# Another written order for the steps of the four mixers in a two-block transformer kernel

## The chip, the cores and the metric

The kernel runs on one core of a Trainium2 chip. The metric is the device time of one execution in microseconds (us); lower is better.

## What is computed

Two blocks act on 512 tokens of 1024 features, in float32. The first block has two layers. Each is a half-weighted SwiGLU network, a mixer, and a second half-weighted SwiGLU network (width 2816):

```python
x = x + 0.5 * swiglu(rmsnorm(x), gate, up, down)
x = x + mixer(rmsnorm(x) @ w_in) @ w_out
x = x + 0.5 * swiglu(rmsnorm(x), gate, up, down)
```

The mixer of layer 0 ("ab") puts a differential attention of 4 heads beside an RWKV-7 recurrence of 8 heads. The mixer of layer 1 ("cd") puts a sparse attention of 8 heads beside an mLSTM of 4 heads. The second block has two layers, each a mixer ("z0", "z1") and a gated network with a causal convolution. Its mixer joins four parts: HGRN2 (4 heads), gated linear attention (4 heads), latent attention (4 heads) and a gated delta rule (4 heads). Every recurrence is computed in chunks of 128 tokens. The delta rules need the inverse of a triangular 128x128 matrix for each head and chunk.

## The kernel before

Everything lives in the core's own memory; only weights, constants and tables are read while it runs. Each weight arrives as a "unit" of 128 x 1024 float32 (512 KB). `wload` issues its transfer on the queue of SyncE (SP) into one of three buffers named `raw`, used in turn. ScalarE (ACT) then rounds it into `whi` (L440) and VectorE (DVE) puts the rest into `wlo` (L442); these are three buffers each, also used in turn. Where a unit is to be kept, the parts are `khi` and `klo` instead. The activations are split the same way into `hi` and `lo`. A product takes three matmuls for each 128 features: hi*whi, lo*whi and hi*wlo. A unit of a wide projection (`fm`, L383, 8 steps over the features) is thus 24 matmuls of 128 x 512; a token-major one (`tm`) has two units and 96 matmuls of 128 x 256.

The networks are long runs of such units. The mixers are chains of small operations that wait for each other, among which wide projections are placed. A chain is a Python generator that puts down some instructions and yields; a step is what lies between two yields. The string of a mixer in `ORDER` names the chain whose next step is put down:

```python
def run(order, make):
    live = {}
    for n in order.split() + list(make):
        if n not in live:
            live[n] = make[n]()
        next(live[n], None)
```

A chain that has ended ignores further steps. The names of "ab" are:

- `p0` to `p3`: `rwkv_prep`, for each pair of heads three wide projections and the preparation of the recurrence (tiles `xm`, `zw`, `pb`).
- `c0` to `c3`: `rwkv_core`, 20 steps for each pair of heads. Steps 2 to 12 hold the triangular inverse (`tri_inv`: `py`, `pz` on PE; `X` on DVE), and steps 15 to 18 the scan over chunks (`pu`, `pS` on PE; `u`, `S` on DVE and ACT).
- `d`: `diff_proj`, eight wide projections with their rotation (`rot`) and then two token-major ones.
- `a`: `diff_attn`, 19 steps: scores (`sc`), transposes (`pT`), values (`po`), then `on` and `oT`. After steps 9 and 18 one half of the tokens is ready for the output projection.
- `o` and `L`: the output projection. `o` takes the part of the features that comes from the recurrence, in 8 steps of 12 matmuls. `L` (`out_last`) takes the other part: step 1 for tokens 0 to 255 and step 2 for tokens 256 to 511, 48 matmuls each, followed for every 128 tokens by the normalisation for the next network (`xn` on DVE, `xT` on PE).

In "cd", `m` and `y` are the mLSTM, `n` the sparse attention, `v`, `g`, `c`, `z` projections. In "z0" and "z1", `g0`, `g1` are the delta rule (22 steps, tiles `dec`, `py`, `pz`, `pu`, `pS`), `h0`, `h1` HGRN2 and `l` the gated linear attention (12 steps, tiles `gw`, `gpa`, `gpo`), `m` the latent attention (24 steps: `mq`, `sc`, `pT` of `mee`, `mpo`). Wide projections are `a0`, `a1` (two units each), `mp` (three), `lp` (two), `dz0`, `dz1`, `ag0`, `ag1`, `bg0`, `bg1` (one) and the token-major `ai` and `bv`.

The written order is not the order on the engines. The program is built with

```python
with tile.TileContext(nc, schedule_with_timeline_sim=True, auto_bufs=True) as tc:
```

so a planner takes it. It runs the instructions against its own durations and picks, for each engine, among those whose inputs it holds to be ready. Its trial runs, which also settle the buffers, pick the one written first; its last run picks the one that is due first by the times of the trial. The written order also sets which of the three `raw` buffers a unit gets, so units keep their written order among themselves. SP's constants and tables are pinned in written order. On the chip each engine then runs its own list in order.

Of the kernel before, what the change touches and what calls it, by code (L numbers as in the profile page):

```python
# [39 lines left out]
class Layout:  # L40
# [134 lines left out]
    def weights(self):  # L175
# [104 lines left out]

ORDER = {
# [18 lines left out]
}  # L300


# [1747 lines left out]
```

## Time and profile before

| quantity | value |
|---|---|
| median of 3 runs | 3824.14 us (3816.77 to 3828.89) |
| the profiled execution, its own time | 3819.23 us |
| its span, first to last instruction | 3817.4 us |
| TensorE (PE) busy with matmuls | 3700.3 us, 97% |
| TensorE's mean granted clock | 0.963 of full speed |
| VectorE, ScalarE, GpSimd busy | 48%, 37%, 7% |

Outside its span the profiled execution has 3819.23 - 3817.4 = 1.8 us. A granted clock of 1.00 is 2.4 GHz and one of 0.50 is 1.2 GHz; a value between is a stretch that has both. In time, "ab" lies at about 424 to 850 us, "cd" at 1640 to 1930, "z0" at 2310 to 2690 and "z1" at 3085 to 3455.

### The profile page before, as it was taken

The numbers are of one execution on the slowest core, as the hardware profiler recorded it, in microseconds if no ns is written. First come the engines' busy times: TensorE is split into PE (matmuls) and PEld (weight loads), VectorE is DVE, ScalarE is ACT, GpSimd is POOL, SyncE is SP. The second block draws the span as 40 slices with busy tenths as digits, with TensorE's granted clock in tenths as the row PEclk, the third lists the DMA queues.
The fourth block names the chain that finished last, engine by engine and source line by source line (L and its number), as shares of the span: only waits on it lengthen the run. The fifth ranks groups of instructions, "written<-read, shape, count | busy, mean of one in ns | idle before, by whom it ended". The sixth has DMA issues, their size and how long they took to land.

```text
span 3817.4 us, 62093 instructions
## 1 busy us (share of the span) xinstructions
PE 3700.3 (97%) x26572; PEld 3023.7 (79%) x26572; DVE 1824.0 (48%) x3017; ACT 1420.5 (37%) x2557; POOL 277.6 (7%) x314
## 2 busy tenths in 40 slices
PE   8999999999999999999999999999999999999999
PEld 7888877778888888877688887767888887678887
DVE  4334645453334333646533357465534664665345
ACT  3223423342223222535432246345332464453323
POOL 0000211100000000010000003121000021210000
PEclk9999999889999999999999999879999999799999
DMA  3223201202222222411022231201222312012222
GB/s 134 100 95 110 74 29 37 67 29 92 96 96 98 100 94 100 137 67 67 1 97 97 99 111 56 65 18 51 83 100 94 127 51 69 20 51 83 94 100 88
DMA packets 88403, 302.97 MB, mean 79 GB/s; under 512 B 9920, under 2 KB 11840, under 8 KB 88128
## 3 DMA queue, kind: packets, MB, share of 16 engines
q1 hardware_dynamic: 88128, 299.01, 22.8%
q8 instruction: 208, 3.41, 0.4%
q14 instruction: 67, 0.55, 0.0%
HBM read 296.87 MB, written 2.10 MB: 78 GB/s over the span
## 4 chain that ended last, share of the span: by engine, by line
PE 88%; DVE 5%; issue 3%; ACT 2%; DMA 1%; POOL 0%; SPq 0%; DVEq 0%; POOLq 0%; ACTq 0%
PE fm L383 54%; PE dn L383 17%; PE tm L383 3%; PE sc L383 2%; PE pu L383 2%; PE ocat L383 1%; PE pT L387 1%; DMA raw<-in_wts_dram 1%; PE gpa L383 1%; PE xT L387 1%; PE py L383 1%; PE pz L383 1%; PE gpo L383 1%; DVE xn L587 0%; DVE klo L442 0%
## 5 line engine op out<-in xcount | busy, mean ns | idle before, releaser
L442 DVE TENSOR_TENSOR wlo<-raw,whi 128x1024 fp32r<-128x1024 f32 x437 | 539.4, 1234 | 981.3 <-ACT whi L440 979.6
L383 PE MATMUL fm<-hi,whi 128*128 128x512 f32 x2456 | 976.2, 398 | 2.8 <-DVE dec L1772 2.8
L383 PE MATMUL fm<-lo,whi 128*128 128x512 f32 x2456 | 970.5, 395 | 0.0
L383 PE MATMUL fm<-hi,wlo 128*128 128x512 f32 x2456 | 968.8, 394 | 0.0
L440 ACT ACTIVATE whi<-raw 128x1024 fp32r<-128x1024 f32 x437 | 463.1, 1060 | 1354.8 <-PE fm L383 596.7
L383 PEld LDWEIGHTS fm<-hi,whi 128*128 128x128 f32 x2456 | 468.9, 191 | 103.6 <-DVE dec L1772 3.0
L383 PEld LDWEIGHTS fm<-hi,wlo 128*128 128x128 f32 x2456 | 468.3, 191 | 97.4
L383 PEld LDWEIGHTS fm<-lo,whi 128*128 128x128 f32 x2456 | 468.3, 191 | 96.9 <-issue 1.0
L383 PE MATMUL dn<-wlo,hi 128*128 128x512 f32 x768 | 299.0, 389 | 0.0
L383 PE MATMUL dn<-whi,lo 128*128 128x512 f32 x768 | 299.0, 389 | 0.0
L383 PE MATMUL dn<-whi,hi 128*128 128x512 f32 x768 | 299.0, 389 | 0.0
L563 POOL TENSOR_TENSOR smalls<-smalls,mhalf 128x1 f32<-128x1 f32 x60 | 42.5, 709 | 2478.0 <-DVE smalls L562 2471.9
L607 DVE TENSOR_TENSOR silu<-silu,fm 128x512 f32<-128x512 f32 x88 | 60.5, 687 | 312.3 <-PE fm L383 312.3
L383 PE MATMUL fm<-lo,khi 128*128 128x256 f32 x640 | 181.5, 287 | 2.2 <-DVE lo L593 2.2
L383 PE MATMUL fm<-hi,khi 128*128 128x256 f32 x640 | 180.5, 288 | 1.0 <-ACT hi L390 0.7
L383 PE MATMUL fm<-hi,klo 128*128 128x256 f32 x640 | 180.5, 285 | 0.0
L383 PEld LDWEIGHTS dn<-whi,lo 128*128 128x128 f32 x768 | 144.2, 188 | 29.9
L383 PEld LDWEIGHTS dn<-whi,hi 128*128 128x128 f32 x768 | 144.2, 188 | 29.8
L383 PEld LDWEIGHTS dn<-wlo,hi 128*128 128x128 f32 x768 | 144.2, 188 | 29.8
L442 DVE TENSOR_TENSOR klo<-raw,khi 128x512 fp32r<-128x512 f32 x184 | 117.4, 684 | 32.5 <-ACT khi L440 32.4
L383 PEld LDWEIGHTS fm<-lo,khi 128*128 128x128 f32 x640 | 123.8, 194 | 4.1 <-DVE lo L593 3.6
L440 ACT ACTIVATE khi<-raw 128x512 fp32r<-128x512 f32 x184 | 103.8, 622 | 59.6 <-DMA raw<-in_wts_dram 56.1
(544 smaller groups left out, 5428.8 us busy)
## 6 DMA issues: line engine op xcount, KB each, us to landing
raw<-in_wts_dram SPq DMA_DIRECT2D x529, 512.0 KB, 3.3
w<-in_small_dram SPq DMA_DIRECT2D x16, 256.0 KB, 5.4
x<-in_x_dram SPq DMA_DIRECT2D x4, 512.0 KB, 6.5
out_dram<-x SPq DMA_DIRECT2D x4, 512.0 KB, 2.6
ffa_norm<-in_small_dram SPq DMA_DIRECT2D x4, 256.0 KB, 6.7
mix_norm<-in_small_dram SPq DMA_DIRECT2D x4, 256.0 KB, 4.1
ropetab<-in_rope_dram SPq DMA_DIRECT2D x4, 256.0 KB, 4.2
ffb_norm<-in_small_dram SPq DMA_DIRECT2D x4, 256.0 KB, 5.6
```

What stands on the lines that cost most here:

```text
L383: self.nc.tensor.matmul(out, lhsT=lhsT, rhs=rhs, start=start, stop=stop, skip_group_check=True)
L387: self.nc.tensor.transpose(out, in_, self.ident[:p, :p])
L440: nc.scalar.activation(t, raw[:, b:e], AF.Copy)
L442: nc.vector.tensor_sub(lo, raw[:, b:e], hi.bitcast(F))
L563: self.nc.gpsimd.tensor_tensor(r, v, self.mhalf, op=OP.pow)
L607: nc.vector.tensor_mul(s, s, pu)
```

## The change

The four strings of `ORDER` are replaced; each has the same names, each as often as before (123, 91, 127 and 127 of them). No other line differs.

- "ab": `c0` is written up to four steps ahead of `c1` instead of in turn with it, and `c2` and `c3` in runs of two or three steps. `p2` comes one step of `c1` earlier. The first three `d` come 3 to 6 steps of `c0` earlier, the sixth to eighth 2 to 4 steps of `c2` later. The tenth `d` comes after step 18 of `c3` instead of step 16. The last three steps of `o` come after step 11 of `a` instead of step 9. Step 1 of `L` comes after step 18 of `a`, straight before step 2, instead of before step 10.
- "cd": three of the `m` steps and one `n` change places by one or two.
- "z0": `a1` moves from before step 3 of `g1` to before its step 10. The first two steps of `o` come after steps 2 and 3 of `m` instead of step 1, the next four one to three steps of `m` later; some `h` and `g` steps change places by one or two.
- "z1": `a1` moves behind step 4 of `g0`. The first six steps of `o` move later in the same way, the last two come one step of `m` earlier, and step 1 of `L` comes after step 16 of `m` instead of 15.

```diff
     "ab":
-        "p1 p0 c0 c1 c0 c1 c0 c1 c0 c1 c0 c1 p2 c0 c1 c0 c1 c0 c1 c0 c1 d c0 c1 c0 c1 c0 c1 c0 c1 d c0 c1 c0 "
-        "c1 c0 c1 c0 c1 d c0 c1 c0 c1 p3 c0 c1 c2 c3 c2 c3 d c2 c3 c2 c3 c2 c3 d c2 c3 c2 c3 d c2 c3 c2 c3 "
-        "c2 c3 d c2 c3 c2 c3 d c2 c3 c2 c3 d c2 c3 c2 c3 d c2 c3 c2 c3 a c2 c3 a c2 c3 a a o a o a o a o a o "
-        "a o o o L a a a a a a a a a a L",
+        "p1 p0 c0 c1 c0 c1 c0 c1 c0 c0 c1 p2 c0 c1 d c0 c1 c0 c1 c1 c0 c0 d c0 c1 d c0 c1 c0 c1 c0 c0 c1 c1 c0 c1 c0 "
+        "c1 p3 c0 c1 c2 c3 c2 c3 c1 c0 c1 c0 c1 c1 d c2 c2 c2 c3 c3 c3 d c2 c2 c3 c3 c2 c2 c3 c2 c2 d c2 c3 c2 c3 c3 "
+        "c3 c2 d d c3 c3 d c2 c3 c2 c3 c2 c3 c2 c2 c3 d a c3 a c2 c3 a a o o a o a a a a o o a a o o o a a a a a a a "
+        "L L a",
     "cd":
-        "m v m m m v m z m z m m z c m c z m c z m c z c z c n m m n m c m m m n n c m m n m g n m n g g n n "
-        "g n n n n y n n o n o n o n o n o n o o o L n n n n n n n n n n n n n n n n n n L",
+        "m v m m m v m z m z m m z c m c m z m c z m c z c z c n n m m m c m m n n c m m n m g n m n g g n n g n n n "
+        "n y n n o n o n o n o n o n o o o L n n n n n n n n n n n n n n n n n n L",
     "z0":
-        "g0 ai g1 a0 g0 g1 g0 a1 g1 g0 g1 g1 g0 g1 mp g0 g1 g0 lp g0 g1 g1 g1 g0 bv g1 g0 dz0 g1 g0 h1 h1 g0 "
-        "h0 g0 g1 dz1 g0 g1 h0 ag1 g1 h1 h0 g0 h0 h1 g1 g0 h0 g1 h1 g0 g1 h0 h0 h0 h1 g0 g1 ag0 bg0 g0 h1 g0 "
-        "h0 g1 bg1 g1 h1 h1 h1 g0 h1 h0 g0 h0 g1 h0 l h1 m o o l m l m o m l m o l m o l l m o m m l m m o l "
-        "m o l m l m l l m L m m m m m m m m m L",
+        "g0 ai g1 a0 g0 g1 g0 g1 g0 g1 g1 g0 g1 g1 mp g0 g0 g1 lp g0 g1 a1 g1 g0 bv g1 g0 dz0 g0 h1 h1 g1 h0 h0 g0 g0 "
+        "g1 dz1 g0 g1 h0 ag1 g1 h1 g0 h0 h0 g1 g0 h0 g1 h1 g0 g1 h0 h1 h0 h1 g0 g1 ag0 bg0 g0 h1 g0 h0 g1 bg1 g1 h1 "
+        "h1 h1 g0 h1 h0 g0 h0 g1 h0 l h1 m l l m o m o m l m o l m o l l m o m m l m o m o l m o l m l m L m m m m m "
+        "m m m m L l",
...
```

## Rows read from the trace of the kernel before

**Rows 1.** The page's head: span, busy time by engine, granted clock in 40 slices.

```profile
span 3817.4 us, 62093 instructions
PE 3700.3 (97%) x26572; PEld 3023.7 (79%) x26572; DVE 1824.0 (48%) x3017; ACT 1420.5 (37%) x2557; POOL 277.6 (7%) x314
PEclk9999999889999999999999999879999999799999
```

**Rows 2.** Windows: start:end and length, busy us (instructions), clock; a network, then ab, cd, z0, z1.

```profile
core 0: us, PE busy (x) PEld busy (x) DVE busy (x) ACT busy (x) POOL busy (x), PEclk, DMA share, GB/s
2000.00:2100.00 100.00, 100.00 (x443) 82.88 (x442) 34.89 (x37) 25.78 (x30) 0.00 (x0) 1.00 0.28 95
424.00:850.00 426.00, 397.54 (x4553) 310.65 (x4552) 225.07 (x462) 164.33 (x367) 67.03 (x68) 0.91 0.12 41
1640.00:1930.00 290.00, 286.18 (x1779) 208.21 (x1778) 154.28 (x349) 135.14 (x333) 20.86 (x26) 0.97 0.14 46
2310.00:2690.00 380.00, 347.59 (x4568) 276.26 (x4567) 217.17 (x447) 182.68 (x385) 76.05 (x77) 0.87 0.14 46
3085.00:3455.00 370.00, 345.53 (x4574) 273.23 (x4573) 219.18 (x448) 184.79 (x388) 75.04 (x77) 0.89 0.14 49
```

**Rows 3.** Windows of thin stretches inside ab, z0 and z1.

```profile
465.00:545.00 80.00, 71.11 (x1431) 58.10 (x1421) 32.66 (x70) 26.52 (x63) 10.58 (x15) 0.89 0.07 22
595.00:643.00 48.00, 40.53 (x1182) 33.17 (x1179) 21.85 (x46) 10.36 (x23) 2.72 (x2) 0.86 0.09 28
697.00:731.00 34.00, 34.00 (x152) 24.36 (x151) 14.10 (x42) 11.93 (x37) 0.00 (x0) 0.65 0.09 32
765.00:835.00 70.00, 63.55 (x309) 45.75 (x307) 37.92 (x85) 29.86 (x80) 3.70 (x5) 0.88 0.00 1
2358.00:2380.00 22.00, 16.43 (x148) 13.01 (x148) 18.33 (x41) 14.07 (x25) 11.99 (x11) 0.84 0.08 25
2471.00:2508.00 37.00, 31.05 (x464) 25.53 (x463) 14.46 (x36) 12.72 (x31) 7.40 (x11) 0.58 0.16 59
2596.00:2611.00 15.00, 9.31 (x256) 7.54 (x244) 8.77 (x22) 11.15 (x32) 1.74 (x2) 0.77 0.59 215
3359.00:3376.00 17.00, 12.85 (x284) 10.14 (x270) 10.72 (x31) 11.39 (x37) 1.72 (x2) 0.65 0.45 167
```

**Rows 4.** Waits of PE: us in total, times, longest.

```profile
PE gpa L383 <- issue: 13.4, 5, 3.7
PE oT L387 <- DVE on L1029: 3.4, 1, 3.4
PE fm L383 <- DVE dec L1772: 2.8, 1, 2.8
PE py L383 <- DVE X L655: 2.7, 1, 2.7
```

**Rows 5.** Chain of waits over ab, in time: start, us, what.

```profile
694.95 7.12 PE tm L383 x59
766.06 9.72 PE sc L383 x21
775.77 13.17 PE fm L383 x48
820.06 13.36 PE fm L383 x48
```

**Rows 6.** Timeline of PE: the recurrence's inverse (py) and the third preparation (zw).

```profile
457.51 0.24 PE L383 MATMUL py<-X,natc 32*32 32x32 f32 x2
462.88 0.69 PE L383 MATMUL zw<-xm,rw_w2a 64*128 64x512 f32 x1
```

**Rows 7.** Waits of the SP queue and of DVE: us in total, times, longest.

```profile
SPq L437 <- DVE wlo L442: 2324.5, 386, 59.8
DVE wlo L442 <- ACT whi L440: 62.7, 15, 10.3
```

10 rows, old and new, of the table ORDER are left out of this document.

## Prediction

> **What bounds the kernel now.** I read the page's head first: PE is busy in 97% of the span and no other engine in half of it [rows 1]. So the time is PE's, and the question is where PE is slower than it has to be. Next the windows by stage. In a network PE runs 443 matmuls in 100 us, 0.226 us each, without idle time and at a clock of 1.00 [rows 2]. An order inside the mixers can't touch that. In the mixers PE has idle time, and its clock falls. Idle time is length less busy: 426 - 397.5 = 28.5 us in ab, 3.8 in cd, 32.4 in z0 and 24.5 in z1, together 89 us. Time at half clock is twice the missing share times the length: 77, 17, 99 and 81 us, together 274 us. If all of that work were bound by the clock, half of the 274 would come back, 137 us. The ceiling of any reordering is then 89 + 137 = 226 us, about 6% of the span.
>
> The busy share hides this. From 697 to 731 us PE reads 34.00 busy of 34.00, yet the clock is 0.65 and it starts 152 matmuls, most of them short [rows 3]. The reader is to see that a busy PE is here one that waits for its own chain. The Trainium skill says so too (Perfetto Trace Analysis, Identifying the Most-Contended Engine): matmul busy time misjudges headroom, and weight-load busy time is better. By that rule, with 0.83 in a network and 310.7/426 = 0.73 in ab [rows 2], ab alone would have about 50 us of headroom, against 28.5 us by idle time; the sum below needs neither.
>
> Why PE is thin there: in the inverse, the scan and the attention each matmul waits for DVE or ACT, which wait for the matmul before. Wide projections, which depend on nothing in the chains, are the only filler. Their amount is fixed. An order can only decide which thin stretch gets them, and which chains overlap.
>
> **The change, part by part.** No instruction is added or removed. All 26572 matmuls [rows 1], all DVE and ACT work and all transfers stay, so every term is idle time or half-clock time gained or lost. I bound a gain by the idle time of a stretch plus half of its half-clock time. The loss side of a moved projection is its own length, should the place that it leaves stay empty.
>
> The end of ab. Step 1 of L now runs as one block of 48 matmuls, 13.2 us, directly after a run of scores (9.7 us, for most of which the clock is low), and the attention of the later tokens follows it without that filler. Then PE waits 3.4 us for `on`, and the second 48 matmuls follow in 13.4 us [rows 4, 5]. Written behind the attention, the first 48 can fill its holes, since they are ready after step 9 of `a`. The stretch from 765 to 835 has 70 - 63.55 = 6.5 us of idle time and 0.12 x 2 x 70 = 16.8 us at half clock [rows 3], so the bound is 6.5 + 8.4 = 15 us. I take 6, about the idle time, because the wait for `on` is the one the block can surely cover. What is late then is the normalisation of tokens 0 to 255, and with it the next network's first matmuls, which fill some holes now.
>
> The end of c2 and c3 (697 to 731): 0.35 x 2 x 34 = 24 us at half clock, no idle time, bound 12 us [rows 3]. The tenth `d`, whose matmuls end just before (59 of its 96 in the 7.1 us from 695 [rows 5]), is written two steps later and so may reach into it. I take 4, a third, since the scan's own waits stay.
>
> The two pairs out of step (465 to 545 and 595 to 643): idle 8.9 + 7.5 = 16.4 us, at half clock 17.6 + 13.4 = 31 us, bound 32 us [rows 3]. When both chains are in the same phase, both wait at once; a few steps apart, the scan of one can lie over the inverse of the other. But the first chains must still start together behind `p1 p0`, and the filler is the same. I take 5, a sixth.
>
> cd: a few steps change places by one, in a stretch with 3.8 us of idle time. Nothing, between -2 and +2.
>
> z0: `a1` (48 matmuls, 48 x 0.226 = 10.8 us) goes from a place where PE has work to the start of the inverse, where it waits 2.8 us for `dec` and 2.7 for `X` [rows 4]. `o` goes towards 2596 to 2611. Together 5.6 + 5.7 us idle and 7.0 + 6.9 at half clock, bound 18 us [rows 3]; I take 4. The thinnest stretch, 2471 to 2508 at a clock of 0.58 [rows 3], holds scans and `gpa` steps, and nothing is moved to it.
>
> z1: `a1` moves by less; the spaced `o` is for 3359 to 3376, 4.2 us idle and 11.9 at half clock, bound 10 us [rows 3]; I take 3.
>
> Sum: 6 + 4 + 5 + 0 + 4 + 3 = 22 us, of bounds that add up to 87. Its loss side: the moved blocks are 13.2 us (L), 11.6 (the tenth `d`, 96 matmuls at 7.12/59 = 0.121 us) and twice 10.8 (`a1`), together 46 us, if each leaves a hole as long as itself.
>
> The transfers move with their steps, all on SP's queue. SP waits 2325 us in 386 waits for a `raw` buffer to come free behind `wlo` [rows 7], so it is always ahead of its use and no load is late today. Moved units keep this: three buffers in written order. The conversions, ACT's and DVE's, go along; DVE waited for ACT's `whi` 62.7 us in ab [rows 7] without being the bound.
>
> The profiled execution took 3819.2 us, 4.9 below the median of the three runs. 3819.2 - 22 is 3797; on the scale of the medians it is 3802. I predict 3800 us.
>
> **The rivals.** The planner undoes it. It picks what is ready, not what is written next: the third preparation, written after step 5 of `c0`, has its `zw` at 462.9 us, 5 us after the first matmuls of step 3 of the inverse work [rows 6]. A hole that `a1` leaves is then filled by the next projection, and the one it moves to was filled anyway. For it: the filler's total is fixed. Against it: it cannot move a unit past another, and its durations are not the chip's, or the holes of rows 4 would not be there. Time: 3824, give or take 11 us.
>
> Slower: a matmul that waits blocks all behind it. On each engine the list runs in order, and PE had waits of up to 3.7 us before `gpa` [rows 4]. The new order puts more unlike chains next to each other in that list; where the planner holds a chain ready sooner than it is, every projection behind it waits too. Its place would be the end of ab: if step 1 of L ends up behind the attention instead of in it, its 13.2 us leave 775, the 6.5 us of idle time stay, and two more normalisations come at the end. It decides as soon as less than half of the block lies in holes. Price: 13 us there, and a second one like it for `a1` (10.8), so 24 us: 3848. The Trainium skill has the rule (TensorE: Matmul & The Clock Gate, The mechanism): matmuls start and end strictly in program order. The trace agrees, as the wait of 3.7 us with nothing started in it shows.
>
> The pairs work as a whole: overlapping unlike phases removes half of the bounds, 44 us, mostly by clock (ab's 77 us at half clock would fall below 50): 3778.
>
> **How the numbers follow.** A measurement of this kernel tells about 0.3% (11.5 us) from no change. The forecast, 3785 to 3812, has 0.44; the larger gain, below 3785, 0.18; the planner's undoing, 3813 to 3835, 0.22; slower, 3836 to 3870, 0.16. Faster is 0.62, same 0.22, slower 0.16. The range leaves out the far half of the larger gain's tail and nearly all of the slower case: 3762 to 3836. The forecast's own range is 3785 to 3812.
>
> **What would show it.** Right: in ab idle time and half-clock time both fall, the 48 matmuls of step 1 of L are spread between scores and values, and the 3.4 us before `oT` are gone; the mean clock rises from 0.963 to about 0.97; in z0 the waits for `dec` and `X` shrink; cd and the networks stay. Wrong: the same waits under other names, a block of 96 matmuls of L after the last `oT`, a longer wait for `xn` at the end of ab, or a lower clock in z0, where `a1` is missed at its old place.

## The result and the profile after

| | before | after |
|---|---|---|
| median of the runs beside each other (4 and 4) | 3820.45 us | 3764.87 us |
| range | 3806.51 to 3828.89 | 3764.24 to 3769.12 |
| ratio, 95% interval | | 0.986 (0.9829 to 0.9892) |
| the profiled execution, its span | 3819.23, 3817.4 | 3765.42, 3763.6 |
| idle time of PE (span less busy) | 117.1 | 95.5 |
| mean granted clock | 0.963 | 0.972 |

The change is 1.4% faster, 56 us by these medians; 22 us were forecast. The head of the page of after answers to [rows 1]:

```profile
span 3763.6 us, 62067 instructions
PE 3668.1 (97%) x26572; PEld 3005.2 (80%) x26572; DVE 1816.6 (48%) x3017; ACT 1418.8 (38%) x2555; POOL 277.2 (7%) x314
PEclk9999999999999999999999999889999999799999
```

PE runs the same 26572 matmuls and is busy for 32 us less, because fewer of them run at half clock, and idle for 21.6 us less. The windows of the four mixers of after answer to [rows 2], here cut where each mixer ends now:

```profile
core 0: us, PE busy (x) PEld busy (x) DVE busy (x) ACT busy (x) POOL busy (x), PEclk, DMA share, GB/s
424.00:814.00 390.00, 374.12 (x4555) 297.48 (x4552) 222.83 (x462) 162.75 (x367) 69.00 (x68) 0.96 0.13 45
1602.00:1892.00 290.00, 286.14 (x1792) 209.87 (x1792) 156.45 (x354) 135.47 (x333) 20.01 (x26) 0.98 0.14 47
2273.00:2647.00 374.00, 346.02 (x4596) 276.78 (x4595) 213.91 (x446) 181.85 (x383) 75.31 (x77) 0.89 0.15 49
3037.00:3403.00 366.00, 345.29 (x4599) 273.82 (x4598) 222.31 (x455) 186.96 (x391) 74.61 (x77) 0.90 0.15 50
```

The number of matmuls shows that each window holds about the same work as its counterpart: 4555 against 4553 in ab. The reader is to read two things in each line, length less busy and the missing clock. In ab the idle time fell from 28.5 to 390 - 374.12 = 15.9 us, and the time at half clock from 77 to 0.04 x 2 x 390 = 31 us. In z0 and z1 both fell a little; cd stayed. A cut that needs no choice says the same: from the last `dn` matmul of one network to the first of the next, ab takes 503.9 us against 539.6 (-36), cd 431.1 against 432.7, z0 493.2 against 502.0 (-9), z1 487.7 against 494.6 (-7).

So ab has two thirds of it. I cut it at three events that both kernels have: the third preparation's `zw`, the fourth one's, the last scan matmul (`pu`), and the last transpose of the normalisation (`xT`). Windows of before, then of after:

```profile
463.00:573.00 110.00, 101.11 (x1686) 80.69 (x1686) 49.46 (x100) 36.96 (x82) 19.55 (x21) 0.92 0.09 31
573.00:722.00 149.00, 141.38 (x2016) 114.34 (x2015) 67.12 (x136) 51.23 (x116) 20.02 (x23) 0.90 0.12 38
722.00:838.00 116.00, 106.20 (x500) 76.36 (x500) 70.94 (x163) 50.31 (x131) 12.10 (x12) 0.90 0.11 37
```

```profile
463.00:555.00 92.00, 88.41 (x1650) 71.58 (x1648) 41.15 (x86) 32.24 (x70) 16.05 (x19) 1.00 0.09 31
555.00:697.00 142.00, 136.11 (x2026) 111.71 (x2023) 67.20 (x138) 48.45 (x109) 23.46 (x25) 0.92 0.10 32
697.00:803.00 106.00, 103.15 (x550) 76.76 (x550) 76.05 (x178) 56.51 (x149) 12.63 (x12) 0.98 0.14 50
```

In these two executions the first part (c0 and c1) is 18 us shorter, the second (c2 and c3) 7 and the end 10. In the first part of after the clock does not fall at all: 1.00. That is one execution: in the profile of ab alone, with the same string, it lies at half clock for 14 of 98 us. The other profiles below bear out the 10, and leave the 18 and the 7 uncertain as sizes.

At the end, step 1 of L is where the forecast wanted it. Its 48 matmuls were one block of 13.2 us at 775 [rows 5]; in the timeline of after they stand in runs of 11, 8, 6, 15, 1 and 7 between transposes (`pT`), values (`po`) and the first normalisation. Some rows of PE (start, length, what, count; the bracket is the idle time before it):

```profile
759.33 0.48 PE L383 MATMUL fm<-khi,hi 128*128 128x512 f32 x1
...
761.93 1.25 PE L387 MATMUL pT<-small,ee 128*128 128x128 f32 x10
762.94 0.48 PE L383 MATMUL fm<-klo,hi 128*128 128x512 f32 x1
...
766.70 3.29 PE L383 MATMUL po<-va,pTs 128*128 128x128 f32 x28
769.83 1.04 PE L387 MATMUL pT<-small,ee 128*128 128x128 f32 x8
770.62 0.48 PE L383 MATMUL fm<-khi,lo 128*128 128x512 f32 x1
...
780.61 0.66 PE L387 MATMUL oT<-small,on 128*128 128x128 f32 x4 [1.38 <-DVE on L1029]
782.53 0.63 PE L387 MATMUL xT<-small,xn 128*128 128x128 f32 x4 [1.26 <-DVE xn L587]
```

The wait for `on` fell from 3.4 us [rows 4] to 1.4, and 1.3 us of waiting for `xn` came in its place. That is the price that was expected of a later normalisation, and it is smaller than the gain.

### The profile page after: what moved, and what is told of

It reads as the page before. It is cut to its first block, busy times and chain, and to the rows that moved or that the text cites. A ratio compares the mean times of both kernels' runs of the same rounds, so it can differ in the third digit from the quotient of the medians.

```text
span 3763.6 us, 62067 instructions
## 1 busy us (share of the span) xinstructions
PE 3668.1 (97%) x26572; PEld 3005.2 (80%) x26572; DVE 1816.6 (48%) x3017; ACT 1418.8 (38%) x2555; POOL 277.2 (7%) x314
## 4 chain that ended last, share of the span: by engine, by line
PE 90%; DVE 5%; ACT 2%; issue 2%; DMA 1%; POOL 0%; SPq 0%; DVEq 0%; POOLq 0%; ACTq 0%
PE fm L383 55%; PE dn L383 17%; PE tm L383 3%; PE sc L383 2%; PE pu L383 2%; PE py L383 1%; PE ocat L383 1%; PE pT L387 1%; PE pz L383 1%; PE gpa L383 1%; PE xT L387 1%; DMA raw<-in_wts_dram 1%; DVE xn L587 0%; PE mpo L383 0%; PE gpo L383 0%
```

## The experiments

Each kernel is before with one part of the new strings or, in the third group, a rearrangement of them. The two theories at the start: each part gains by its own overlap (A), or every rewritten order draws a new schedule from the planner and the time moves by luck (B). A third, C, came with the fifth run.

**Which mixer.** The new string of ab alone; then those of cd, z0 and z1 alone.

```diff
 "ab":
-    (before)
+    (after)
```

> Only ab has the new order. Where the parts act by themselves (theory A: each mixer gains by its own overlap), ab keeps the 36 us that its stretch between the networks lost in the profile of after (539.6 to 503.9 us), and the time is about 3785 us, ratio 0.990 to 0.992. If the planner's choices all over the program hang together (theory B: luck of one whole schedule), ab's stretch lies 10 us or more away from 504 us.

> Only cd, z0 and z1 have the new orders. Theory A: their stretches as in after (431, 493 and 488 us), 16 us less in all, about 3804 us, ratio about 0.996; ab stays at 540 us. Theory B: stretches 10 us or more from those, or ab moves too.

Measured: 0.9915 (0.9887 to 0.9943), and 0.9941 (0.9916 to 0.9966). The product is 0.9857, the whole change's 0.986. So the two times multiply to the whole. The stretch of ab in the profile is 507.4 us in the first run, as A had it. In the second those of cd, z0 and z1 are 429.4, 490.6 and 489.9 us, near what A had; ab's is 549.4 us, where ab was unchanged and 540 was expected. In the first run z1, though unchanged, takes 504.0 us instead of 494.6. Both are told below.

**Which part of ab.** The new order up to step 4 of `a`, and the new order behind it.

```diff
 head: (after up to the fourth a)
-   ... a a o o a o a a a a o o a a o o o a a a a a a a L L a
+   ... a a o a o a o a o a o a o o o L a a a a a a a a a a L
 end:  (before up to the fourth a)
-   ... a a o a o a o a o a o a o o o L a a a a a a a a a a L
+   ... a a o o a o a a a a o o a a o o o a a a a a a a L L a
```

> ab with the new order up to step 4 of a and the old one behind it (o and a in turn, L before step 10 of a). If the pairs out of step and the held-back d make the gain, as the whole up to the last scan matmul (697 us in after against 722 in before) suggests, ab gains about 25 us of its 36 and its stretch is about 515 us. By the forecast's own terms it would be 9 us.

> ab with the old order up to step 4 of a and the new one behind it (L behind step 18 of a). By the traces (116 us from the last scan matmul to the last transpose of the normalisation in before, 106 in after) it gains about 10 us, stretch about 529 us; by the forecast 6; by the rival of a waiting block at the end it loses up to 13 and is at 553.

Measured: 0.9929 (0.9903 to 0.9956), and 0.9958 (0.9933 to 0.9983). Each helps by itself, 27 and 16 us. Whether they add is not resolved: the product, 0.9887, would be better than ab as a whole, but the intervals overlap. The stretches of ab in the profiles are 536.2 and 538.7 us, where 515 and 529 were expected. The profiled execution of the head is the slowest of its ten (3816.71 us), with ab at half clock for 92 us; in that of the end the first part, with the old order, takes 125 us instead of 110. The end itself, from the last `pu` to the last `xT`, takes 102 us there instead of 116, with 5.7 us of idle time instead of 9.8:

```profile
736.00:838.00 102.00, 96.28 (x495) 70.96 (x495) 70.35 (x163) 49.69 (x131) 12.26 (x12) 0.97 0.13 42
```

**Stagger or places.** The new order with each pair in turn again; the old order with the stagger alone; and a control, the old order with the names within each pair exchanged.

```diff
 after, in turn:
-... c0 c1 c0 c0 c1 p2 c0 c1 d c0 c1 c0 c1 c1 c0 c0 d c0 c1 d ... c1 d c2 c2 c2 c3 c3 c3 d c2 c2 c3 c3 c2 c2 c3 ...
+... c0 c1 c0 c1 c0 p2 c1 c0 d c1 c0 c1 c0 c1 c0 c1 d c0 c1 d ... c1 d c2 c3 c2 c3 c2 c3 d c2 c3 c2 c3 c2 c3 c2 ...
 before, staggered:
-... c0 c1 c0 c1 c0 c1 p2 c0 c1 c0 c1 c0 c1 c0 c1 d c0 c1 c0 c1 c0 c1 c0 c1 d ...
+... c0 c1 c0 c0 c1 c0 p2 c1 c0 c1 c0 c1 c1 c0 c0 d c0 c1 c0 c1 c0 c1 c0 c0 d ...
 before, exchanged:
-p1 p0 c0 c1 c0 c1 ... c2 c3 c2 c3 d ...
+p1 p0 c1 c0 c1 c0 ... c3 c2 c3 c2 d ...
```

> The new order of ab, but with c0 and c1 in turn and c2 and c3 in turn in the same places; p, d, a, o and L stay where the new order has them. If the stagger within a pair makes the gain of the first part (theory A), only the end's gain is left: ratio about 0.996. If the places of the projections and the early start of c2 and c3 beside the end of c0 and c1 make it (theory C), the ratio is that of the new ab, about 0.9915.

> The old order of ab with the stagger alone: the places of the chain steps are the old ones, filled with the new sequence of c0 and c1 and then of c2 and c3; p, d, a, o, L stay in their old places. Theory A: about 0.993, as the first part of the new order gave. Theory C: 1.000.

> A control: the old order of ab with the names c0 and c1 exchanged, and c2 and c3. The same filler and the same phases, only another list from the planner. If each rewritten order moves the time by the planner's luck (theory B), it is 0.4% or more away from 1; theories A and C say 0.998 to 1.002.

Measured: 0.9927 (0.9907 to 0.9947), 0.9928 (0.9911 to 0.9944), 0.9994 (0.997 to 1.0018). The control is 1, though PE's list in ab differs from before's in 617 of 5172 places. So a new list alone does not bring 0.7% in ab, as far as one control can show, and B falls as the cause of ab's gain. A and C are each half right: each foretold one of the first two results and missed the other. Windows of the three parts of ab, first of the run in turn, then of the run with the stagger alone:

```profile
465.00:562.00 97.00, 89.39 (x1604) 71.47 (x1600) 40.63 (x81) 32.66 (x70) 15.19 (x16) 0.92 0.08 29
562.00:724.00 162.00, 155.03 (x2062) 127.27 (x2060) 66.19 (x140) 49.88 (x110) 22.76 (x28) 0.82 0.09 28
724.00:828.00 104.00, 101.15 (x548) 75.25 (x548) 75.97 (x177) 55.94 (x148) 12.36 (x12) 1.00 0.14 51
```

```profile
462.00:570.00 108.00, 104.37 (x1711) 83.34 (x1708) 50.11 (x104) 36.75 (x82) 18.46 (x20) 0.92 0.09 31
570.00:719.00 149.00, 142.93 (x2019) 115.16 (x2018) 66.58 (x138) 51.77 (x117) 21.56 (x23) 0.90 0.11 38
719.00:833.00 114.00, 103.88 (x500) 75.43 (x499) 70.78 (x163) 50.46 (x131) 12.07 (x12) 0.92 0.11 38
```

In these profiles the first part takes 97 us with the places alone, 108 with the stagger alone (and its idle time falls from 8.9 to 3.6 us), 92 with both. In the second part the run in turn takes 162 us at a clock of 0.82, against 142 in after. That the new places need the stagger there is not shown: of the 34 us more at half clock, some 20 come from one spell of 24 us at the last scan matmuls, and the head of ab, which has the stagger, shows the same spell in its profile.

**Which part of z0 and z1.** Only the part behind the first step of `l` (`m`, `l`, `o`, `L`); only `a1`; only the part before the first step of `l`, which has `a1` and the shifted `h` and `g` steps.

```diff
 "z0", a1 alone:
-"g0 ai g1 a0 g0 g1 g0 a1 g1 g0 g1 g1 g0 g1 mp g0 g1 g0 lp g0 g1 g1 g1 g0 bv ...
+"g0 ai g1 a0 g0 g1 g0 g1 g0 g1 g1 g0 g1 mp g0 g1 g0 lp g0 g1 g1 a1 g1 g0 bv ...
 "z0", behind l:
-... h0 l h1 m o o l m l m o m l m o l m o l l m o m m l m m o l m o l m l m l l m L ...
+... h0 l h1 m l l m o m o m l m o l m o l l m o m m l m o m o l m o l m l m L ...
```

> z0 and z1 with the new order behind the first step of l (m, l, o, L), the old one before it. The forecast gave this part 7 less what a1 does, about 4 to 5 us: 0.9985. If all of the 22 us that cd, z0 and z1 gained together come from here, 0.994; if from a1 and the h and g steps, 1.000.

> The old orders with a1 alone moved in z0 and z1, to its new place. The part behind the first step of l gave nothing (1.0025), so the 22 us of the three later mixers lie before it. If a1 is their cause, as the forecast had it (4 us of z0's gain came from it), 0.994 to 0.996; if the h and g steps are, 1.000.

> z0 and z1 with the new order before the first step of l (a1 and the shifted h and g steps), the old one behind it. If the parts act by themselves, the whole gain of the later mixers: 0.992 to 0.995. If head and end only work together, 0.998 or more.

Measured: 1.0025 (1.0003 to 1.0046), 0.9966 (0.994 to 0.9992), 0.9977 (0.9952 to 1.0003). `a1` alone gains about 13 us (3 to 23). The profiles show what it removes: in the five kernels that have `a1` in its new place, PE shows no wait for `dec` before a wide projection and none for `X` in the inverse, in z0 or z1. In each of the nine others one or both mixers have 1 to 6 us of these waits (5.5 in z0 of before [rows 4]). The spaced `o` by itself gains nothing. Head and end together gave 0.9941 with cd; the product of the two alone would be 1.000. That they gain only together is still not shown: the last run below has the head and cd on top of another kernel, without the new end, and is 18 us faster than that kernel.

**Everything that helped by itself.** The stagger in the old places with the new end; then that with the new heads of z0 and z1 and the new cd.

```diff
 "ab": before, staggered, up to the fourth a
-   ... a a o a o a o a o a o a o o o L a a a a a a a a a a L
+   ... a a o o a o a a a a o o a a o o o a a a a a a a L L a
```

> ab with the stagger alone in the old places and the new order behind step 4 of a. If the two are independent, the product of their ratios, 0.9928 x 0.9958 = 0.9886, better than the new ab (0.9915). If a thin stretch can only be filled once, about the new ab's 0.9915.

> ab as in the run with stagger and end, z0 and z1 with the new order before the first step of l alone, cd new. If the parts add up it beats the change: 0.9886 x 0.993 = 0.982, about 3757 us; if they do not, 0.986 as the change.

Measured: 0.9939 (0.9918 to 0.996) and 0.9902 (0.9868 to 0.9937). Stagger and end do not add, and neither kernel is better than the change. In the profiles the end of ab is shorter with both than with the stagger alone (105 us against 114), but z1, whose string is the same, takes 505.9 us against 492.8. From the first kernel to the second it is 18 us (3804.21 to 3785.81), about what `a1` gave by itself.

**The mixers whose string did not change.** The planner draws the whole program anew each time. Eight profiles have the old string of z0 and eight that of z1. The stretch of z0 lies between 486.5 and 504.1 us in them, that of z1 between 492.8 and 509.2, with PE idle for 23 to 33 and 24 to 34 us. PE's lists differ from before's in 67 to 368 of 5257 places in z0. How much of the spread is list and how much is clock is not separated. Either way theory B's luck, some 10 us in each of these mixers, is there, and it is as large as the 9 and 7 us of z0 and z1 in after. The gain of the end of ab by itself has it too: z0 takes 486.5 us in that profile instead of 502.0. The five profiles with `a1` moved have 488 to 493 us in z1, at the low end of the old range or below it, and 491 to 501 in z0, which can't be told from the old. Only ab is clear of this luck: 503.9 and 507.4 us with its whole new string, 539.6 to 553.8 in the five profiles with the old.

**The same list, another time.** The runs of the kernel before that stood beside these (69 of them, on three chips) spread from 3806 to 3847 us. Each has its mean clock, 0.955 to 0.967, and a straight line through them is 7069.8 - 3375.1 x clock, with a correlation of -0.96. At equal clock the runs can be compared much more closely. Below is the mean distance of each kernel's runs from that line, and PE's idle time in the profile (span less busy on the page):

| kernel | ratio | median clock | us from the line | idle us |
|---|---|---|---|---|
| before | 1 | 0.960 | 0 | 117.1 |
| exchanged names | 0.9994 | 0.962 | +1 | 117.1 |
| z0, z1 behind l | 1.0025 | 0.958 | +1 | 117.2 |
| z0, z1 before l | 0.9977 | 0.961 | -6 | 116.6 |
| a1 alone | 0.9966 | 0.963 | -9 | 109.7 |
| stagger alone | 0.9928 | 0.964 | -9 | 108.2 |
| end of ab | 0.9958 | 0.962 | -9 | 107.4 |
| ab in turn | 0.9927 | 0.963 | -13 | 110.0 |
| cd, z0, z1 | 0.9941 | 0.963 | -13 | 104.8 |
| stagger and end of ab | 0.9939 | 0.965 | -9 | 102.6 |
| all that helped alone | 0.9902 | 0.968 | -19 | 99.4 |
| ab | 0.9915 | 0.967 | -14 | 102.2 |
| head of ab | 0.9929 | 0.966 | -16 | 100.7 |
| after | 0.986 | 0.972 | -26 | 95.5 |

The distance at equal clock goes roughly with the idle time (-26 us against -21.6 for after; the row of z0 and z1 before `l`, -6 against -0.5, fits worst). The rest of the gain is clock: 0.972 - 0.960 = 0.012, times 3375 gives 40 us. Together that is 66 us below the median of these 69 runs, 3828.8; the four runs beside after were lower, 3820.45.

Where the clock is won or lost can be seen in the first part of ab. The run with z0 and z1 behind `l` has the list of before in ab: PE's differs in 2 of 5172 places, those of DVE, ACT and GpSimd in none. Yet it takes 128 us for the first part instead of 110. The runs of `a1` alone, of z0 and z1 before `l` and of cd, z0 and z1 have this list of PE too: 111, 128 and 127 us. Windows of that run, the whole first part and the same 48 us inside it; then those 48 us in the profile of before:

```profile
463.00:591.00 128.00, 119.33 (x1688) 97.32 (x1686) 48.47 (x100) 36.66 (x82) 20.63 (x21) 0.76 0.08 26
514.00:562.00 48.00, 46.67 (x261) 39.91 (x262) 11.86 (x31) 6.28 (x15) 2.60 (x4) 0.50 0.04 12
```

```profile
514.00:562.00 48.00, 48.00 (x357) 37.96 (x355) 16.90 (x45) 8.94 (x22) 5.00 (x7) 0.89 0.07 23
```

In both the clock falls at 514 us, while or just after PE waits 1.66 us for ACT behind `ropex`, a step of the rotation of `d`. In before it is back in a few us (and falls once more, for 7 us, at 538); in the other run it stays at 0.50 for all of the 48 us, and 261 matmuls start instead of 357. It comes back at 562 us, while the next wide projection runs, and so it does in the other profiles in which it stayed low as long. Rows of PE in that run (the duration of a 128x512 matmul falls from 0.63 to 0.40 us with the rise):

```profile
515.33 1.05 PE L383 MATMUL pz<-y,XT 32*32 32x32 f32 x16 [1.66 <-ACT ropex L390]
...
561.00 0.63 PE L383 MATMUL fm<-hi,wlo 128*128 128x512 f32 x1
561.43 0.59 PE L383 MATMUL fm<-hi,whi 128*128 128x512 f32 x1
561.85 0.40 PE L383 MATMUL fm<-lo,whi 128*128 128x512 f32 x1
```

Of the seven profiles with the old list or nearly so in this part, five took 125 to 128 us and two 110 or 111; the one that the prediction read is one of the two. With the stagger, the new head or both, the seven profiles took 91 to 108 us.

## Why the prediction was right, and where it was too small

The direction was right, and the time lies at the low edge of the range of 3762 to 3836. The likeliest case, 22 us, was too small, and the time is outside its own range of 3785 to 3812. What came is nearest to the rival that the prediction gave 0.18: the pairs working as a whole, mostly by clock, with ab's time at half clock below 50 us (31, and 38 in the profile of ab alone). Its reason is borne out in part only: no part of the new ab came below 50 in its profile (55 to 92). That the time lies 3 us inside the range is luck, since nothing in the sum of 22 us leads there. Of the signs named beforehand the 48 matmuls are spread, idle and half-clock time fell in ab, the mean clock is 0.972, and the waits for `dec` and `X` [rows 4] are gone from z0 (1.6 us for `dec` came there at another place, before `pkk`); the 3.4 us before `oT` fell to 1.4 and are not gone.

**What bounds it.** Right. The reasoning from idle time and half-clock time holds in numbers: the line through 69 runs makes 0.01 of mean clock, which is 76 us at half clock, worth 34 us, 44% of it, against the half that the ceiling assumed. The Trainium skill's rule on weight-load busy time (Perfetto Trace Analysis, Identifying the Most-Contended Engine) gave about 50 us of headroom in ab; the trace agrees as to the side, since ab lost 36 us and its weight-load share rose from 0.73 to 297.5/390 = 0.76.

**The end of ab.** Mechanism right, size too small: 6 taken, 10 in the profiles (the end takes 102 to 108 us in the six profiles with its new order, 112 to 124 in the eight others), 16 in the run by itself (6 to 26), not all of it from ab. The bound was 15. I took the idle time alone; the clock of that part rose too, from 0.90 to 0.98.

**The end of c2 and c3.** 4 taken; the second part of ab was 7 us shorter than in before, but five profiles with the old list of PE have 145 to 149 us there, against 142. After the change the tenth `d` lies among the scan's matmuls, and the clock there is 0.95 instead of 0.65 [rows 3]:

```profile
665.00:699.00 34.00, 34.00 (x286) 30.82 (x286) 9.31 (x24) 7.08 (x19) 3.45 (x5) 0.95 0.10 32
```

The place of `d` alone does not do this. In the profile of the head of ab it lies in the same way (15, 19 and 62 of its matmuls around the last `pu`), and the clock is as low as before. So the term came out, but not for the reason given alone; what else keeps the clock up in after and in the run of ab alone stays open:

```profile
676.00:710.00 34.00, 34.00 (x212) 29.93 (x212) 5.58 (x18) 3.61 (x12) 2.23 (x5) 0.65 0.04 14
```

**The two pairs out of step.** This is the step that failed in size. A sixth of a bound of 32 us was taken, 5, for both pairs; the first pair alone gave 18 in the profiles, and more against the 125 to 128 us that the old list mostly takes. The bound came from one execution, and from one of the short ones. The reason given, unlike phases over each other, is half of it: with earlier projections and the pairs in turn the first part is about as short (97 us). How either of them keeps the clock from staying low there is not shown.

**cd** gave 1.6 us, nothing to speak of, as forecast. **z0 and z1**: 4 and 3 taken, 9 and 7 in the profiles, which is no more than their unchanged strings vary by. `a1` was right as a mechanism, since the waits for `dec` and `X` went, and its own run gave more than thought (13 us in both, 3 to 23). That `o` fills 2596 to 2611 and 3359 to 3376 was wrong as a term of its own.

**The transfers.** SP stayed ahead: it waits 2457 us behind `wlo` now, in 394 waits, against 2325 in 386 [rows 7].

**The rivals.** The planner undoes it: no, though its choices reach far; in the run with ab alone, PE's list in z0 differs from before's in 368 of 5257 places, and z1 is 9 us longer. A waiting block at the end of ab: it did not come. Left open: what head and end of z0 and z1 are worth apart from the planner's luck, and why the clock, once it has fallen at 514 us, comes back soon in one execution and late in another.

## What to carry to other kernels

Where one engine is busy 97% of the time and its clock depends on what it does, look for stretches that are busy and short of work at once: few matmuls started, clock below 1. Wide, independent work belongs there, written after what it is to fill the holes of. Parts that gain alone need not add, and a planner that takes the whole program can give back in an untouched stage what a change gains in its own; so look at the untouched stages too, over several kernels. When runs of one kernel differ, set their time against the mean clock first; here the 69 runs lie 3 us from their line, so at equal clock a few runs tell about 5 us apart in 3800.

## What the runs showed of the hardware

One list of PE took 110 or 111 us for the same part in two profiles and 127 or 128 in three, by whether the clock, once at 0.50, came back in a few us or stayed there for 44 to 48. PE is 97% busy while it stays low (46.67 of 48 us; the profile models the ends of matmuls), so no idle gap holds it down. The fall itself comes within 2 us of a wait of PE, 1.66 us behind `ropex`, in all five. The Trainium skill (TensorE: Matmul & The Clock Gate, HAM oscillation) puts the loss of clock down to gaps in which PE is idle; here the fall at 514 us agrees, and the measurement differs in two things: the clock stayed low without a gap, and from 697 to 731 us, with 34.00 of 34.00 busy, it fell without one (0.65 [rows 3]).
